# The gate and up products of a feed-forward block by one level of Strassen's scheme

## The chip, the core and the metric

The kernel runs on one core of a Trainium2 chip. The metric is the device time of one execution in microseconds (us). TensorE (PE in the rows) multiplies matrices into PSUM; VectorE (DVE), ScalarE (ACT) and GpSimd (POOL) work element by element; SyncE (SP) issues the transfers between DRAM and SBUF. Each engine runs its own list of instructions in order and waits at semaphores for the others.

## The reference

One decoder block for 1024 tokens of width 1024: two parallel mixers, a merge, an output product and a norm, and then the feed-forward part with which this change deals. In the reference's words:

```
h = h + rms_norm(mixed, mix_post_g[l])
u = rms_norm(h, ffn_pre_g[l])
gt, up = jnp.split(u @ w_ffn_in[l], 2, axis=-1)
h = h + rms_norm((jax.nn.silu(gt) * up) @ w_ffn_out[l], ffn_post_g[l])
```

`gt` and `up` are each 1024 x 2816, and `w_ffn_out` brings 2816 back to 1024. All is float32.

## The kernel before

Float32 products are made of three TensorE products each. An operand is split into a rounded high part and the remainder, its low part (`split`, line 83: ACT casts the high part at line 84, DVE subtracts it at line 85), and high x high, high x low and low x high are added in PSUM (`stat3`, line 101; `mov3`, line 106). A weight unit of 128 x 1024 is a DMA of 512 KB into `wr` and such a split into `wh` and `wl` (`unit`, line 87).

Before the feed-forward part stands the output product of the mixers (`wo_job`), for three sets of tokens (a "token" here is a block of 128): 0 to 2, 3 to 5, 6 and 7. While TensorE makes one set, `after` norms the tokens of the set before. For each token that is: sum of squares on ACT (line 981), the reciprocal root in two tiny POOL instructions (lines 97 and 98, tile `rs`), scale and residual on DVE (984, 985), `h2` to DRAM, sum of squares again (989), `rs` again, the scale to `n` on DVE (993), eight 128x128 transposes on TensorE (999), and the split of their results into `u2h` and `u2l`, which hold the normed activations transposed: 8 chunks of the width x 1024 tokens. Tokens 6 and 7 have no later set to hide behind. There `early` fills TensorE with 48 matmuls of hidden chunk 0, which need only tokens 0 to 3 (tile `f`).

The hidden width is 22 chunks of 128. For each chunk `gate_part` and `up_part` make a gate and an up product of 8 (chunks of the width) x 2 (token halves) x 3 = 48 matmuls 128x128 by 128x512, in the order of `chan_gen`: for each weight piece both token halves after one another. Silu (ACT, 1071), the product of gate and up (DVE, 1082) and its split follow. Every group of two chunks (the last has four) then passes through `out_part`, which multiplies it with `w_ffn_out` (line 1127) and adds the PSUM result to the accumulators `acc` on DVE (1114). The last group norms and writes the result.

Each engine's list is the order in which the program is written, with `drive` weaving a filler generator into the steps of a main one by numbers of nanoseconds. Nothing is rearranged later. So an instruction that stands in a list waits for all that stand before it there, also where it doesn't use their results.

Of the kernel before, what the change touches and what calls it, by code (L numbers as in the profile page):

```python
# [17 lines left out]
P = 128  # L18
D = 1024
# [23 lines left out]
def _f(ap):  # L43
    return ap.bitcast(F32)
# [3 lines left out]
def block_kernel(ctx: ExitStack, tc: tile.TileContext, a: dict, out: bass.AP, dbg=None):  # L48
# [84 lines left out]
    gb_d = dram("gb", [8, P, T])  # L133
    ma_d = dram("ma", [8, P, T])
    h2_d = dram("h2", [NT, P, D])

    HW = ((0, 512), (512, 1024))

# [767 lines left out]
    def yb_job(j):  # L906
        def run(w):
            gm, ma = io("gb"), io("ma")
            SP.dma_start(gm, gb_d[j])
            SP.dma_start(ma, ma_d[j])  # L910
            box = []
            yield from chan_gen(box, w, bh_, bl_)
            DVE.scalar_tensor_tensor(out=v2(gm), in0=v2(gm), scalar=1.0, in1=box[0], op0=ALU.add, op1=ALU.mult)
            DVE.tensor_tensor(out=gm, in0=gm, in1=ma, op=ALU.add)
            h_ = mp.tile([P, T], F32R, name=f"mh{j}", tag=f"mh{j}")
            l_ = mp.tile([P, T], F32R, name=f"ml{j}", tag=f"ml{j}")
            ACT.activation(h_, gm, AF.Copy, scale=0.5)
            DVE.scalar_tensor_tensor(out=l_, in0=gm, scalar=0.5, in1=_f(h_), op0=ALU.mult, op1=ALU.subtract)
            mh.append(h_)
            ml.append(l_)  # L920

        return (lambda: unit(a["wmo"][j])), run

# [7 lines left out]
    drain(G)  # L931
    pYa.close()
    bh_, bl_ = resident(ybp, ob_d, "b")
    pM = ExitStack()
    mp = pM.enter_context(tc.tile_pool(name="mp", bufs=1, reuse_waits="tile"))
    mh, ml = [], []
    drain(stream([yb_job(j) for j in range(8)]))
    pYb.close()


    fp = ctx.enter_context(tc.tile_pool(name="fp", bufs=1, side="right", reuse_waits="tile"))
    u2h = fp.tile([P, KC, T], F32R, name="u2h", tag="u2h")
    u2l = fp.tile([P, KC, T], F32R, name="u2l", tag="u2l")
    wo = pM.enter_context(tc.tile_pool(name="wo", bufs=1, reuse_waits="tile"))
# [4 lines left out]
    mix = {}  # L949

    def wo_job(toks, ch, k2, outs, spare):
        def run(w):
            wh, wl = (z.rearrange("p (k m) -> p k m", k=2) for z in w)
            if k2 == 0:
                if ch == 0:
                    b = [big("wo") for _ in range((len(toks) + 1) // 2)]
                    b = [z[:, i] for z in b for i in range(2)]
                    outs[:], spare[:] = b[: len(toks)], b[len(toks) :]
                else:
                    outs[:] = spare + [bank("wo2") for _ in toks[len(spare) :]]  # L960
            for i, t in enumerate(toks):
                xs = slice(t * P, (t + 1) * P)
                for k in range(2):
                    kc = 2 * k2 + k
                    mov3(outs[i], mh[kc][:, xs], ml[kc][:, xs], wh[:, k], wl[:, k], kc == 0, kc == KC - 1)
                if k2 == 3:
                    if ch == 0:
                        mix[t] = wo.tile([P, D], F32, name="mx", tag="mx", bufs=4)
                    ACT.copy(mix[t][:, 512 * ch : 512 * ch + 512], outs[i])
                yield 1290  # L970

        return (lambda: unit(a["wout"][ch, k2])), run

    def after(tok):
        m = mix.pop(tok)
        jk = u2l[:, :, tok * P : (tok + 1) * P]
        m8 = m.rearrange("p (k c) -> p k c", k=KC)
# [17 lines left out]
        c0 = tok * P  # L995
        for g in range(2):
            pt = bank("x2").rearrange("p (k c) -> p k c", c=P)
            for kc in range(4):
                PE.transpose(pt[:, kc], n[:, (4 * g + kc) * P : (4 * g + kc + 1) * P], ident)
            split(u2h[:, 4 * g : 4 * g + 4, c0 : c0 + P], u2l[:, 4 * g : 4 * g + 4, c0 : c0 + P], pt)  # L1000

    pipe = []

# [33 lines left out]
    def half_gen(w, b, e, o):
        wh, wl = (z.rearrange("p (k m) -> p k m", k=KC) for z in w)
        for kc in range(KC):
            stat3([o], wh[:, kc], wl[:, kc], [u2h[:, kc, b:e]], [u2l[:, kc, b:e]], kc == 0, kc == KC - 1)  # L1040
            yield 650

    w0 = [unit(a["wfg"][0]), unit(a["wfu"][0])]
    o0 = [big("f0") for _ in range(2)]
# [8 lines left out]
    for i in range(2):  # L1053
        drain(half_gen(w0[i], *HW[1], o0[i][:, 1]))
    pM.close()

    gp = ctx.enter_context(tc.tile_pool(name="gp", bufs=1, reuse_waits="tile"))
    acc = [gp.tile([P, D], F32, name=f"acc{t}", tag=f"acc{t}") for t in range(NT)]
    ends = list(range(GROUP, NH - 2 * GROUP + 1, GROUP)) + [NH]
    groups = [list(range(b, e)) for b, e in zip([0] + ends, ends)]  # L1060
    acts, sls = {}, {}

    def gate_part(j):
        s = gp.tile([P, 2, 512], F32, name="sl", tag="sl", bufs=2)
        if j == 0:
            o = o0[0]
        else:
            box = []
            drain(chan_gen(box, unit(a["wfg"][j]), halves(u2h), halves(u2l)))
            o = box[0]  # L1070
        ACT.activation(s, o, AF.Silu)
        sls[j] = s

    def up_part(j):
        s = sls.pop(j)
        if j == 0:
            o = o0[1]
        else:
            box = []
            drain(chan_gen(box, unit(a["wfu"][j]), halves(u2h), halves(u2l)))  # L1080
            o = box[0]
        DVE.tensor_tensor(out=s, in0=s, in1=o, op=ALU.mult)  # L1082
        ah = gp.tile([P, 2, 512], F32R, name="ah", tag="ah", bufs=4)
        al = gp.tile([P, 2, 512], F32R, name="al", tag="al", bufs=4)
        split(ah, al, s)
        acts[j] = ah, al

    def unit2(src):
        raw = wp.tile([P, 1024], F32, name="wr", tag="wr", bufs=3)
        hi = gp.tile([P, 1024], F32R, name="w2h", tag="w2h", bufs=2)  # L1090
        lo = gp.tile([P, 1024], F32R, name="w2l", tag="w2l", bufs=2)
        SP.dma_start(raw, src)
        split(hi, lo, raw)
        return hi, lo

    def out_part(gi):
        grp = groups[gi]
        last = gi == len(groups) - 1
        if last:
            gf = gp.tile([P, 2, 512], F32, name="sl", tag="sl", bufs=2)  # L1100
            SP.dma_start(gf.rearrange("p a c -> p (a c)"), a["ffn_post_g"].partition_broadcast(P))
        ws = [(unit2 if i < 2 else unit)(a["wfo"][j]) for i, j in enumerate(grp)]
        late = []
        for t in range(NT):
            bs = [bank("f2") for _ in range(2)]
# [4 lines left out]
            def add(ch):  # L1110
# [4 lines left out]
                if last:  # L1115
                    ACT.activation(jk[:, 512 * ch : 512 * ch + 512], av[ch], AF.Square, accum_out=s2[:, ch : ch + 1])

            pieces = ((0,), (1,)) if last and t == NT - 1 else ((0, 1),)
            for chs in pieces:
                for i, jj in enumerate(grp):  # L1120
                    xs = slice((t % 4) * P, (t % 4) * P + P)
                    ahs, als = (z[:, t // 4, xs] for z in acts[jj])
# [41 lines left out]
def _stationary(w):  # L1164
# [74 lines left out]
```

## Time and profile before

| | |
|---|---|
| median of 3 runs | 2064.35 us (2064.09 to 2065.51) |
| the profiled execution | 2065.24 us |
| its span (first to last instruction) | 2063.4 us |
| granted clock of TensorE, mean over the span | 0.997 of full speed |
| TensorE busy | 2029.8 us, 98% |
| VectorE, ScalarE, GpSimd busy | 979.6, 584.6, 81.6 us |
| DMA | 163 MB, 79 GB/s on average |
| end of the norms to the last matmul | 1330 to 2054.8 us of the span |

A stretch in which TensorE is busy all the time and its matmuls follow one another at an even distance is set by the number of matmuls. A stretch in which it waits is set by the chain of engines that it waits for. Rows of the trace give the start of an instruction, its duration, and in brackets the idle time before it with what ended it.

### The profile page before, as it was taken

How to read it: one execution, taken by the hardware profiler on the slowest of the kernel's cores; microseconds unless marked ns; L12 is line 12 of the kernel's file. 1: busy time of each engine (PE TensorE's matmuls, PEld its weight loads, DVE VectorE, ACT ScalarE, POOL GpSimd, SP SyncE). 2: the span in 40 equal slices, each digit the busy share in tenths (PEclk: the TensorE clock that was granted, in tenths of full speed). 3: DMA queues.
4: the chain of work that ended last, by engine and by line, in shares of the span. 5: the costliest groups of instructions: out<-in, count | busy, mean ns of one | idle time of the engine just before them, and what ended most of it. 6: DMA issues, size and time to landing. Idle time of an engine off the chain costs nothing.

```text
span 2063.4 us, 26451 instructions
## 1 busy us (share of the span) xinstructions
PE 2029.8 (98%) x11044; PEld 1753.0 (85%) x11044; DVE 979.6 (47%) x1707; ACT 584.6 (28%) x978; POOL 81.6 (4%) x149
## 2 busy tenths in 40 slices
PE   7999999999999999999999999999999999999998
PEld 7999998998888888888888887888888888888886
DVE  5456565555443335777762445731432334333326
ACT  5212111211213235555551214632111111111112
POOL 1000000000001100000000001200000000000002
PEclk9999999999999999999999999999999999999999
DMA  4111111021213033111145654621111111121014
GB/s 166 52 42 42 51 43 41 22 62 41 91 56 115 21 118 118 47 52 47 37 153 198 205 153 161 218 80 51 51 41 52 51 52 43 40 62 51 22 60 153
DMA packets 54151, 163.08 MB, mean 79 GB/s; under 512 B 5376, under 2 KB 14080, under 8 KB 54032
## 3 DMA queue, kind: packets, MB, share of 16 engines
q1 hardware_dynamic: 53888, 161.13, 23.8%
q8 instruction: 87, 1.43, 0.3%
q14 instruction: 32, 0.26, 0.0%
q10 hardware_dynamic: 144, 0.26, 0.0%
HBM read 127.82 MB, written 33.55 MB: 78 GB/s over the span
## 4 chain that ended last, share of the span: by engine, by line
PE 59%; issue 35%; DVE 2%; ACT 1%; POOL 1%; DMA 1%; SPq 0%; POOLq 0%; DVEq 0%; ACTq 0%
PE gm L104 25%; PE vb L108 6%; PE sb L750 3%; PE fb L104 3%; PE wo L108 3%; PE cb L108 3%; PE ov L811 2%; PE lv L367 2%; PE pT L798 1%; PE fg L104 1%; PE qn L104 1%; PE dg L306 1%; PE kn L104 1%; PE ob L427 1%; PE ob L426 1%
## 5 line engine op out<-in xcount | busy, mean ns | idle before, releaser
L84 ACT CAST wh<-wr 128x1024 fp32r<-128x1024 f32 (+1 forms) x143 | 148.7, 1040 | 695.3 <-PE gm L104 377.7
L85 DVE TENSOR_TENSOR wl<-wr,wh 128x1024 fp32r<-128x1024 f32 (+1 forms) x143 | 172.4, 1207 | 283.4 <-ACT wh L84 269.0
L104 PE MATMUL gm<-u2h,wl 128*128 128x512 f32 x672 | 206.9, 389 | 0.0
L104 PE MATMUL gm<-u2h,wh 128*128 128x512 f32 x672 | 206.9, 389 | 0.0
L104 PE MATMUL gm<-u2l,wh 128*128 128x512 f32 x672 | 206.9, 389 | 0.0
L104 PE MATMUL gm<-uh,wh 128*128 128x512 f32 x512 | 164.4, 402 | 0.0
L104 PE MATMUL gm<-uh,wl 128*128 128x512 f32 x512 | 158.3, 390 | 0.0
L104 PE MATMUL gm<-ul,wh 128*128 128x512 f32 x512 | 158.2, 390 | 0.0
L104 PEld LDWEIGHTS gm<-u2h,wl 128*128 128x128 f32 x672 | 126.2, 188 | 26.1
L104 PEld LDWEIGHTS gm<-u2h,wh 128*128 128x128 f32 x672 | 126.2, 188 | 26.1
L104 PEld LDWEIGHTS gm<-u2l,wh 128*128 128x128 f32 x672 | 126.2, 188 | 26.1
L1114 DVE TENSOR_TENSOR acc<-acc,f 128x512 f32<-128x512 f32 x144 | 92.5, 683 | 76.9 <-PE f L1127 76.9
L104 PEld LDWEIGHTS gm<-ul,wh 128*128 128x128 f32 x512 | 96.1, 188 | 20.5
L104 PEld LDWEIGHTS gm<-uh,wl 128*128 128x128 f32 x512 | 96.0, 188 | 20.5
L1082 DVE TENSOR_TENSOR sl<-sl,gm 128x1024 f32<-128x1024 f32 x21 | 25.6, 1221 | 174.1 <-PE gm L104 174.1
L104 PEld LDWEIGHTS gm<-uh,wh 128*128 128x128 f32 x512 | 92.8, 188 | 16.2
L1127 PE MATMUL f<-w2h,ah 128*128 128x512 f32 x320 | 98.9, 389 | 0.0
L1127 PE MATMUL f<-w2h,al 128*128 128x512 f32 x320 | 98.9, 389 | 0.0
L1127 PE MATMUL f<-w2l,ah 128*128 128x512 f32 x320 | 98.8, 389 | 0.0
L108 PE MATMUL vb<-wh,uh 128*128 128x256 f32 (+1 forms) x288 | 84.1, 292 | 0.0
L108 PE MATMUL vb<-wl,uh 128*128 128x256 f32 (+1 forms) x288 | 81.8, 284 | 0.1
L370 DVE COPY_PREDICATED AT<-masks,lv 128x128 f32<-128x128 uint8 x192 | 51.6, 322 | 63.9 <-PE lv L367 61.9
(329 smaller groups left out, 4029.4 us busy)
## 6 DMA issues: line engine op xcount, KB each, us to landing
wr<-in_wout SPq DMA_DIRECT2D x24, 512.0 KB, 3.5
wr<-in_wfg SPq DMA_DIRECT2D x22, 512.0 KB, 3.6
wr<-in_wfu SPq DMA_DIRECT2D x22, 512.0 KB, 3.4
wr<-in_wfo SPq DMA_DIRECT2D x22, 512.0 KB, 3.3
xt<-in_x SPq DMA_DIRECT2D x16, 512.0 KB, 4.8
wr<-in_wv SPq DMA_DIRECT2D x8, 512.0 KB, 3.6
wr<-in_whf SPq DMA_DIRECT2D x8, 512.0 KB, 3.7
wr<-in_whq SPq DMA_DIRECT2D x8, 512.0 KB, 3.6
```

Source lines behind the costliest of these rows:

```text
L84: ACT.copy(hi, src)
L85: DVE.tensor_tensor(out=lo, in0=src, in1=_f(hi), op=ALU.subtract)
L104: PE.matmul(o, w, x, start=first and j == 0, stop=last and j == 2)
L108: PE.matmul(o, x, w, start=first and j == 0, stop=last and j == 2)
L306: PE.matmul(b[:, c], k[:, (2 * g + c) * P : (2 * g + c + 1) * P], qq[:, 2 * g + c], start=True, stop=True)
L367: PE.matmul(b[:, :, c], k[:, cc * P : (cc + 1) * P], qx[:, :, cc], start=True, stop=True)
L370: DVE.copy_predicated(AT[:, 2 * g : 2 * g + 2].rearrange("p c (n w b) -> p (c n) w b", w=2, b=w)[:, :, 1], masks[:, j + s_ + (j > 2)].rear ...
L750: PE.matmul(o, x[:, qs], y[:, b0:e0], start=j == 0, stop=j == 4 and e0 <= d0)
L811: PE.matmul(ov[:, x], w, r[:, x], start=False, stop=kt == nkt - 1 and j == 2)
L1082: DVE.tensor_tensor(out=s, in0=s, in1=o, op=ALU.mult)
L1114: DVE.tensor_tensor(out=av[ch], in0=av[ch], in1=bs[ch], op=ALU.add)
L1127: PE.matmul(bs[ch], x, w[:, 512 * ch : 512 * ch + 512], start=f and j == 0, stop=l and j == 2)
```

## The change

**The products.** Hidden chunk j is paired with chunk j + 11, the two halves of the tokens (tokens 0 to 3 and 4 to 7) and the two halves of the width make a 2 x 2 grid, and a "chain" is one such pair for gate or for up: 22 chains. One level of Strassen's scheme in Winograd's form makes a chain of seven products instead of eight. A product is 4 (chunks of a half width) x 3 = 12 matmuls of 128x512 (`product`, line 1140 of the changed kernel), and several of the seven are added in the same PSUM bank: products 1, 6, 7, 4 in one half of `pa`, product 2 in the other, 5 and 3 in `pc`. In between, `post` copies intermediate results to SBUF on ACT and adds on DVE.

**The sums of weights.** Four sums or differences 128x512 for each chain (line 1111), on POOL for chains 0 and 1 (the gate and up of the first pair), on DVE for the other 20, and then the splits.

**The sums of activations.** For tokens 0 to 3 the normed `n` goes to DRAM as well (`n_d`). For tokens 4 to 7 `after` reads back the token four before into `no`, and POOL makes four differences 128x512 (line 1010, tiles `nt` and `no`); then 20 transposes (line 1022) instead of 8, five pairs of split instructions instead of two.

**The second product.** Silu(gate) x up goes to DRAM (`act_d`), and the product with `w_ffn_out` becomes a stage of its own after all chains; its operands are loaded and split one group ahead.

**The tiles of the mixers' output** are cut into three pools by token sets, so that each of the 8 merged chunks is cast in three pieces on ACT and three on DVE instead of one each.

On POOL, the list at the end of the norms stood as pairs of `rs` instructions. `no` and `nt` are the differences of activations (`n_11757` and `n_11831` are tokens 4 and 5, `n_11980` and `n_12044` tokens 6 and 7), `wr<-wr` the sums of weights:

```order
+L1111 TENSOR_TENSOR wr<-wr 128x512
 L97 TENSOR_SCALAR rs<-ss 128x1
 L98 TENSOR_TENSOR rs<-rs,mhalf 128x1
 L97 TENSOR_SCALAR rs<-ss 128x1
 L98 TENSOR_TENSOR rs<-rs,mhalf 128x1
+L1111 TENSOR_TENSOR wr<-wr 128x512
 L97 TENSOR_SCALAR rs<-ss 128x1
 L98 TENSOR_TENSOR rs<-rs,mhalf 128x1
+L1111 TENSOR_TENSOR wr<-wr 128x512 x2
+L1010 TENSOR_TENSOR nt<-n_11980,no 128x512
+L1010 TENSOR_TENSOR nt<-n_11980,nt 128x512
+L1010 TENSOR_TENSOR no<-nt,no 128x512
```

The three pairs of `rs` are the first norm of token 7, the second of token 6 and the second of token 7. Ahead of these rows stand the four differences of token 4 (with a pair of `rs` between them), the four of token 5, and four sums of weights with the first `rs` pair of token 6 among them; behind them the rest of token 6's differences and the four of token 7. So the `rs` pairs of tokens 6 and 7 now stand behind work on 128x512 tiles, and token 6's differences behind all eight sums of weights.

On TensorE, before, around the transposes of tokens 6 (`n_11854`) and 7 (`n_11887`):

```order
L104 MATMUL f_11798<-u2h,wl 128x512
L999 MATMUL x_11873<-ident,n_11854 128x128 x4
L999 MATMUL x_11880<-ident,n_11854 128x128 x4
L104 MATMUL f_11798<-u2h,wh 128x512
L104 MATMUL f_11798<-u2l,wh 128x512
L104 MATMUL f_11798<-u2h,wl 128x512
L104 MATMUL f_11798<-u2h,wh 128x512
L104 MATMUL f_11798<-u2l,wh 128x512
L104 MATMUL f_11798<-u2h,wl 128x512
L999 MATMUL x_11895<-ident,n_11887 128x128 x4
L999 MATMUL x_11902<-ident,n_11887 128x128 x4
L104 MATMUL f_11797<-u2h,wh 128x512
```

And in the changed kernel, from the last of the 48 matmuls that need no late token:

```order
L1140 MATMUL pa<-xbh,wl 128x512
L1022 MATMUL x_12009<-ident,n_11980 128x128 x4
L1022 MATMUL x_12016<-ident,nt 128x128 x4
L1022 MATMUL x_12023<-ident,nt 128x128 x4
L1022 MATMUL x_12030<-ident,no 128x128 x4
L1022 MATMUL x_12037<-ident,no 128x128 x4
L1022 MATMUL x_12061<-ident,n_12044 128x128 x4
L1022 MATMUL x_12068<-ident,nt 128x128 x4
L1022 MATMUL x_12075<-ident,nt 128x128 x4
L1022 MATMUL x_12082<-ident,no 128x128 x4
L1022 MATMUL x_12089<-ident,no 128x128 x4
L1140 MATMUL pc<-xth,wh 128x512
```

Before, 42 of the fillers stood ahead of token 6 and six between the two tokens. Now all 48 stand ahead of token 6, and the first matmul of product 5 (`pc`) stands behind the last transpose of token 7.

The diff, cut to its core:

```diff
-            h_ = mp.tile([P, T], F32R, name=f"mh{j}", tag=f"mh{j}")
-            l_ = mp.tile([P, T], F32R, name=f"ml{j}", tag=f"ml{j}")
...
+            for (b, e), (h_, l_) in mx_:
+                ACT.activation(h_[:, j], gm[:, b:e], AF.Copy, scale=0.5)
+                DVE.scalar_tensor_tensor(out=l_[:, j], in0=gm[:, b:e], scalar=0.5, in1=_f(h_)[:, j], op0=ALU.mult, op1=ALU.subtract)
...
         n = io("n2")
+        if tok >= 4:
+            o = io("no")
+            SP.dma_start(o, n_d[tok - 4])
         DVE.scalar_tensor_tensor(out=n, in0=m, scalar=r, in1=gpre, op0=ALU.mult, op1=ALU.mult)
+        if tok >= 4:
+            tt = io("nt")
+            o2, n2, t2 = (z.rearrange("p (a c) -> p a c", a=2) for z in (o, n, tt))
+            for out_, x, y in ((t2[:, 0], n2[:, 0], o2[:, 0]), (t2[:, 1], n2[:, 1], t2[:, 0]), (o2[:, 0], t2[:, 1], o2[:, 0]), (o2[:, 1], o2[:, 1], t2[:, 1])):
+                POOL.tensor_tensor(out=out_, in0=x, in1=y, op=ALU.subtract)
+        else:
+            SP.dma_start(n_d[tok], n)
         yield
...
+        def prep(self, part):
+            r0, r1 = (z.rearrange("p (a c) -> p a c", a=2) for z in self.raw)
+            sub = lambda o, x, y, op=ALU.subtract: (POOL if self.n < 2 else DVE).tensor_tensor(out=o, in0=x, in1=y, op=op)
+            if part == 0:
+                self.put(self.raw[0], (1, 2))
+            elif part == 1:
+                z = raw_tile()
+                self.s12 = z.rearrange("p (a c) -> p a c", a=2)
+                sub(self.s12[:, 0], r1[:, 0], r1[:, 1], ALU.add)
+                sub(self.s12[:, 1], self.s12[:, 0], r0[:, 0])
+                self.put(z, (5, 6))
+            elif part == 2:
+                z = raw_tile()
+                s34 = z.rearrange("p (a c) -> p a c", a=2)
+                sub(s34[:, 0], r0[:, 0], r1[:, 0])
+                sub(s34[:, 1], r0[:, 1], self.s12[:, 1])
+                self.put(z, (7, 3))
+            else:
+                self.put(r1[:, 1], (4,))
...
+            for k in range(HK):
+                for j, (w, x) in enumerate(((wh, xh), (wh, xl), (wl, xh))):
+                    PE.matmul(o, w[:, k], x[:, k], start=fresh and k == 0 and j == 0, stop=k == HK - 1 and j == 2, skip_group_check=not fresh)
+                yield 680
+            self.post(i)
...
+    c0.load()
+    for i in range(3):
+        c0.prep(i)
+    c1.load()
+    c1.prep(0)
...
     def early():
-        for i in range(2):
-            yield from half_gen(w0[i], *HW[0], o0[i][:, 0])
+        for c in (c0, c1):
+            yield from c.product(1)
+            yield from c.product(2)
...
+            c.prep(1)
+            yield from c.product(1)
+            yield from chains[n - 1].product(4)
+            c.prep(2)
+            if not last:
+                chains[n + 1].load()
+            yield from c.product(2)
+            yield from c.product(5)
+            c.prep(3)
+            yield from c.product(6)
+            if not last:
+                chains[n + 1].prep(0)
+            yield from c.product(3)
+            yield from c.product(7)
...
-    for gi, grp in enumerate(groups):
-        for i, j in enumerate(grp):
-            gate_part(j)
-            if i == 0 and gi:
-                out_part(gi - 1)
-            up_part(j)
-    out_part(len(groups) - 1)
+    for gi in range(len(groups)):
+        out_part(gi)
```

`put` splits a tile and keeps its two halves as the left operands of two products; `load` reads the two weight chunks of a chain; `big` has two buffers of two PSUM banks, `bank` four of one, and `io` (which holds `n`, `no`, `nt` and the gate tiles) is a ring of SBUF tiles that are used again in turn.

## Rows read from the trace of the kernel before

**Rows 1.** Page, first part: busy us, share of the span, instructions.

```profile
PE 2029.8 (98%) x11044; PEld 1753.0 (85%) x11044; DVE 979.6 (47%) x1707; ACT 584.6 (28%) x978; POOL 81.6 (4%) x149
```

**Rows 2.** Stretches: length, then the columns that the first line names.

```profile
core 0: us, PE busy (x) PEld busy (x) DVE busy (x) ACT busy (x) POOL busy (x), PEclk, DMA share, GB/s
1320.00:1333.00 13.00, 13.00 (x70) 10.99 (x69) 11.51 (x12) 9.23 (x15) 1.25 (x2) 1.00 0.91 324
...
1358.30:2012.00 653.70, 653.70 (x2885) 541.51 (x2884) 204.14 (x231) 112.96 (x118) 0.00 (x0) 1.00 0.15 48
```

**Rows 3.** FFN products, groups by line and shape: busy us, mean ns, idle us.

```profile
L1114 DVE TENSOR_TENSOR acc<-acc,f 128x512 f32<-128x512 f32 x144 | 92.5, 683 | 76.9 <-PE f L1127 76.9
...
L85 DVE TENSOR_TENSOR wl<-wr,wh 128x1024 fp32r<-128x1024 f32 x43 | 52.5, 1222 | 166.7 <-ACT wh L84 166.7
L84 ACT CAST wh<-wr 128x1024 fp32r<-128x1024 f32 x43 | 45.3, 1054 | 371.7 <-PE gm L104 232.0 <-issue 136.4 <-PE f L104 3.3
...
L1071 ACT ACTIVATE sl<-gm 128x1024 f32<-128x1024 f32 x21 | 21.3, 1014 | 0.0
```

**Rows 4.** TensorE in order of time, end of the norms: start, duration.

```profile
1330.18 1.03 PE L999 MATMUL x<-ident,n 128*128 128x128 f32 x8
...
1333.54 0.40 PE L104 MATMUL f<-u2l,wh 128*128 128x512 f32 x1
...
1342.62 0.39 PE L104 MATMUL f<-u2h,wl 128*128 128x512 f32 x1
1342.89 1.06 PE L999 MATMUL x<-ident,n 128*128 128x128 f32 x8
...
1346.45 0.73 PE L104 MATMUL f<-u2h,wh 128*128 128x512 f32 x2 [0.24 <-ACT u2h L84]
```

**Rows 5.** VectorE in order of time, the same place.

```profile
1321.83 1.28 DVE L993 SCALAR_TENSOR_TENSOR n<-mx,rs,gpre 128x1024 f32<-128x1024 f32 x1
...
1335.13 1.28 DVE L85 TENSOR_TENSOR u2l<-x,u2h 128x512 fp32r<-128x512 f32 x2
...
1337.46 1.28 DVE L984 SCALAR_TENSOR_TENSOR mx<-mx,rs,gpost 128x1024 f32<-128x1024 f32 x1
1338.66 1.22 DVE L85 TENSOR_TENSOR wl<-wr,wh 128x1024 fp32r<-128x1024 f32 x1
1339.80 1.22 DVE L985 TENSOR_TENSOR mx<-mx,xt 128x1024 f32<-128x1024 f32 x1
```

**Rows 6.** GpSimd in order of time, the same place.

```profile
1323.58 0.71 POOL L97 TENSOR_SCALAR rs<-ss 128x1 f32<-128x1 f32 x1 [4.73 <-ACT u2l L989]
...
1335.84 0.55 POOL L98 TENSOR_TENSOR rs<-rs,mhalf 128x1 f32<-128x1 f32 x1
1338.88 1.05 POOL L97 TENSOR_SCALAR rs<-ss 128x1 f32<-128x1 f32 x1 [2.49 <-ACT u2l L989]
1340.01 1.41 POOL L98 TENSOR_TENSOR rs<-rs,mhalf 128x1 f32<-128x1 f32 x1
```

**Rows 7.** GpSimd's widest operation in the whole span, by line and shape.

```profile
L474 POOL CAST masks<-tt 128x896 uint8<-128x896 f32 x1 | 0.9, 929 | 0.0
```

**Rows 8.** ScalarE groups of the norms and splits, by line and shape.

```profile
L84 ACT CAST u2h<-x 128x512 fp32r<-128x512 f32 x16 | 8.6, 595 | 1.5 <-PE x L999 1.5
...
L989 ACT ACTIVATE u2l<-mx 128x1024 fp32r<-128x1024 f32 x8 | 8.5, 1062 | 10.0 <-DVE mx L985 8.3 <-POOL rs L97 1.8
```

**Rows 9.** Page, sixth part: DMA issues, count, KB each, median us to landing.

```profile
wr<-in_wfu SPq DMA_DIRECT2D x22, 512.0 KB, 3.4
```

**Rows 10.** TensorE in order of time where its clock rises at the start.

```profile
17.55 0.40 PE L108 MATMUL vb<-wh,ul 128*128 128x256 f32 x1
17.76 0.30 PE L108 MATMUL vb<-wh,uh 128*128 128x256 f32 x1
17.90 0.28 PE L108 MATMUL vb<-wl,uh 128*128 128x256 f32 x1
18.02 0.28 PE L108 MATMUL vb<-wh,ul 128*128 128x256 f32 x1
```

More of the change, by code (lines that the diff above doesn't have):

```diff
@@ L949, in block_kernel, with wide @@
     mix = {}
+    sums = []
+    def wide(name):
+        return wo.tile([P, D], F32, name=name, tag="mx", bufs=4)
     def wo_job(toks, ch, k2, outs, spare):
@@ L1028, in block_kernel @@
     drain(stream(wo_jobs(sets[0])))
+    pM[0].close()
     G = stream(wo_jobs(sets[1]))
@@ L1031, in block_kernel @@
     drain(G)
+    pM[1].close()
+    tp = tp_.enter_context(tc.tile_pool(name="tp", bufs=1, side="right", reuse_waits="tile"))
+    sums[:] = (tp.tile([P, 4, HK, 512], F32R, name=z, tag=z) for z in ("xth", "xtl"))
     G = stream(wo_jobs(sets[2]))
@@ L1034, in block_kernel, with raw_tile @@
     drain(G)
[L1037 to L1044, printed above, removed]
+    pM[2].close()
+    wq = ctx.enter_context(tc.tile_pool(name="wq", bufs=1, reuse_waits="tile"))
+    made = {"r": 0, "u": 0}
+    def raw_tile():
+        made["r"] += 1
+        if made["r"] % 5 < 3:
+            return wp.tile([P, 1024], F32, name="wr", tag="wr", bufs=3)
+        return wq.tile([P, 1024], F32, name="wr", tag="wr", bufs=2)
@@ L1052, in block_kernel, with rest @@
     drain(G)
[L1053 to L1058, printed above, removed]
+    def rest():
+        yield from c0.product(5)
+        c0.prep(3)
+        yield from c0.product(6)
+        c1.prep(1)
+        yield from c0.product(3)
+        yield from c0.product(7)
+        c1.prep(2)
+        chains[2].load()
+        yield from c1.product(5)
+        c1.prep(3)
+        yield from c0.product(4)
+        yield from c1.product(6)
+        chains[2].prep(0)
+        yield from c1.product(3)
+        yield from c1.product(7)
+        for n in range(2, 2 * NP_):
+            c, last = chains[n], n == 2 * NP_ - 1
+            c.prep(1)
[12 more added lines that the diff above has]
+            yield from c.product(7)
+        yield from chains[-1].product(4)
@@ L1088, in unit2, with second @@
[L1088 to L1092, printed above, removed]
-        split(hi, lo, raw)
-        return hi, lo
+    held = {}
+    def second(j, kind, tiles):
+        raw = raw_tile()
+        SP.dma_start(raw, (act_d if kind == "a" else a["wfo"])[j])
+        hi, lo = tiles()
+        split(hi, lo, raw)
+        held[kind, j] = hi, lo
@@ new lines, in block_kernel, with ring @@
+    R = rest()
+    steps = 4 * (7 * 2 * NP_ - 4) - 12
+    for _ in range(steps):
+        next(R)
+    second(0, "a", unit_tiles)
+    drain(R)
+    for kind, j in (("w", 0), ("a", 1), ("w", 1)):
+        second(j, kind, unit_tiles)
+    tp_.close()
+    xp_.close()
+    gp = ctx.enter_context(tc.tile_pool(name="gp", bufs=1, side="right", reuse_waits="tile"))
+    acc = [gp.tile([P, D], F32, name=f"acc{t}", tag=f"acc{t}") for t in range(NT)]
+    def ring():
+        return [gp.tile([P, 1024], F32R, name=z, tag=z, bufs=8) for z in ("vh", "vl")]
@@ L1098, in out_part @@
         last = gi == len(groups) - 1
+        todo = [] if last else [(j, kind) for j in groups[gi + 1] for kind in "aw"]
         if last:
-            gf = gp.tile([P, 2, 512], F32, name="sl", tag="sl", bufs=2)
+            gf = wide("gf").rearrange("p (a c) -> p a c", a=2)
             SP.dma_start(gf.rearrange("p a c -> p (a c)"), a["ffn_post_g"].partition_broadcast(P))
-        ws = [(unit2 if i < 2 else unit)(a["wfo"][j]) for i, j in enumerate(grp)]
+        xs_ = [held.pop(("a", j)) for j in grp]
+        ws = [held.pop(("w", j)) for j in grp]
         late = []
@@ L1116, in add @@
                     ACT.activation(jk[:, 512 * ch : 512 * ch + 512], av[ch], AF.Square, accum_out=s2[:, ch : ch + 1])
+            for _ in range(2 if len(todo) > 4 or t % 2 == 0 else 0):
+                if todo and t < 7:
+                    second(*todo.pop(0), ring)
             pieces = ((0,), (1,)) if last and t == NT - 1 else ((0, 1),)
             for chs in pieces:
[L1120 to L1122 removed]
+                for i in range(len(grp)):
+                    xs = slice(t * P, (t + 1) * P)
+                    ahs, als = (z[:, xs] for z in xs_[i])
                     f, l = i == 0, i == len(grp) - 1
```

150 lines of the change are left out of this document (106 added, 44 removed).

## The prediction, made before the changed kernel ran

> **What bounds the kernel now.** I read the page's first part, then the table of stretches, then the groups by line, then the three engines in order of time where the norms end. TensorE is busy 98% of the span [rows 1]. From 1358 us to 2012 us it is busy in every microsecond: 2885 matmuls in 653.7 us, one every 0.2266 us, while VectorE works 31% of that time, ScalarE 17%, GpSimd not at all, and the DMA engines 15% [rows 2]. So the feed-forward products are bound by the number of matmuls, and a matmul taken away there is worth 0.2267 us. Before that stretch lies a different place. When the output product of the mixers ends (1330.18, transposes of token 4 [rows 4]) TensorE lives on 48 fillers until the last tokens are normed, and the main work starts at 1346.45. Today the fillers cover that chain almost to the end: the wait at 1346.45 is 0.24 us [rows 4]. There VectorE is nearly full, 11.5 of 13 us, and the DMA engines 91% [rows 2].
>
> **Matmuls removed.** Before: 22 chunks x 2 x 48 = 2112 for gate and up. After: 22 chains x 7 products x 12 = 1848. The second product stays at 22 x 8 x 2 x 3 = 1056. So 264 fewer, 264 x 0.2267 = 59.85 us, all on the path. A product accumulates in one bank, where before two banks took turns. The fillers `f` also stay in one bank: 1333.54 to 1342.62 for 40 of them, 0.227 us each [rows 4], so the price of one matmul doesn't change.
>
> **Hand-overs in the chains.** A gate chain takes 84 x 0.2267 = 19.0 us of TensorE. VectorE: four weight sums at 0.68, three and a half low halves at 1.22, three adds at 0.68, 9 us; for an up chain four multiplications at 0.68 more, 12 us. ScalarE: three and a half casts at 1.05, three copies at 0.59, Silu 2.0 for a gate, 7.5 us [rows 3, 8]. Neither is a bound. The tightest hand-over is the copy after product 6, which product 7 waits for since it adds in the same bank: product 3 lies between, 12 x 0.2267 = 2.72 us, and ScalarE answers in 0.59, or in 1.65 if it has just begun a cast. I cost these at nothing; the cover is that one product, and without it each chain would pay some 1.7 us. The second product as a stage needs per group of two chunks 96 matmuls, 21.8 us, against four low halves and sixteen adds on VectorE, 15.8 us [rows 3]; again nothing. Its first operands are loaded within the last chains; for that seam and the one at the end I take 1 us. The extra transfers (22 x 512 KB out and in) come to 35 GB/s beside 48 in a stretch with a DMA share of 15% [rows 2]: nothing. The finer casts of the mixers' output add two short instructions on each of two engines per chunk, beside 48 matmuls (10.9 us): nothing.
>
> **The end of the norms** is where the change costs. It puts 24 instructions of 128x512 on GpSimd (sixteen differences of activations, eight sums of weights), in one line with the `rs` pairs that the norms wait for, and lets TensorE run all 48 fillers first. The trace has no two-input operation of that size on GpSimd. Its widest is a one-input cast, 896 elements in 0.929 us, 1.04 ns per element [rows 7]. At that rate 512 elements take 0.53 us; with two inputs read one after the other, 1.06. A third bound is a difference that first waits for a whole VectorE instruction of 1.28 us [rows 5], 2.34 together. I take 1.06, the rate of the only wide row with both inputs counted, and keep 0.53 and 2.34.
>
> The path, by these rows, with the order of the lists:
> - The `n` of token 4 ends at 1321.83 + 1.28 = 1323.1 [rows 5]. Four differences with the `rs` of token 5 between them (0.71 and 0.55 [rows 6]): 1328.6. Token 5's four: 1332.9.
> - Three sums of weights, `rs` of token 6 (0.19 and 0.55 [rows 6]) with a fourth sum inside: 1337.8. Only now is the transfer of the next weight chunk issued, since it reuses the tile that this sum frees; 3.4 us [rows 9]: 1341.2. The fifth sum waits for it, and the `rs` of token 7 stands behind: 1343.0.
> - VectorE has the scale of token 7 ahead of the residual of token 6, so both tokens wait: 1.28 + 1.22 [rows 5], 1345.5. Square on ScalarE 1.06 [rows 8], `rs` 0.74: 1347.3.
> - The sixth sum, `rs` of token 7, two sums: 1351.3. Token 6's four differences: 1355.5.
> - The `n` of token 7 reuses a tile which those four read, and on VectorE stands behind the split of their transposes (0.4 + 0.60 + 0.64 [rows 4, 5, 8]): 1357.1, then 1.28: 1358.4. Four differences: 1362.7. Four transposes: 1363.2, product 5.
>
> All 24 GpSimd instructions lie on this path, 25.4 us of its 40. Nothing fills TensorE: the 48 fillers (10.9 us) are used up early, and every transpose stands behind them. To it comes contention. An `rs` pair takes 0.19 + 0.55 us alone or beside a split that reads PSUM, as at 1335.84 beside the split of 1335.13. Beside VectorE's instructions with two inputs in SBUF, at 1338.66 and 1339.80, it takes 1.05 + 1.41 [rows 5, 6]: 0.86 more in each. Six low halves of weights, all with two inputs in SBUF, lie off the path in this stretch: 6 x 0.86 = 5.2 us. With some 0.1 us at each of about ten changes of engine: 1369.9. Against 1346.45 that is 23.5 us lost. The 24 additional transposes of tokens 6 and 7 are inside it; those of tokens 4 and 5 run while GpSimd is the later one.
>
> [...]
>
> After such a wait TensorE's clock is at its lower level at first. [...] Between none and all twelve of product 5 I take seven: 1.3 us (0 to 2.2).
>
> **Sum**, against the profiled execution's 2065.24 us: - 59.85 + 23.5 + 1.3 + 1.0 = 2031.2. That execution is 0.9 above the median of the runs, so 2030 us.
>
> **Rivals.**
> *A shorter wait.* At 0.53 us per GpSimd instruction the path loses 24 x 0.53 = 12.7 us: 2018. With everything hidden only the 48 transposes at 0.13 us stay: 2065.2 - 59.9 + 6.2 - 0.9 = 2011. For it: TensorE reads nothing of GpSimd's but these tiles. Against: two inputs, and the waits for the transfer and for the tile of `n` remain at any speed. 2011 to 2022.
> *GpSimd shut out by VectorE.* If each of the 24 first waits for an instruction of 1.28 us, + 30.7: 2061. For it the doubled `rs` rows and VectorE at 88% [rows 2]; against it that VectorE stands on this path itself and can't run beside all of them. 2042 to 2061.
> *The chains wait (the other side).* ScalarE's list holds, ahead of the copies that free a bank, casts of weight sums which wait for VectorE, and VectorE's sums stand behind adds that wait for a product. If that ring closes, TensorE pays in every chain. The 35 us won are gone at 35 / 22 = 1.6 us per chain; at 2 us it is 2030 + 44 = 2074. For it: seven dependent hand-overs where before a product of 48 matmuls had another bank pair free. Against it: 1.1 us of room at the tightest, 7 us of idle VectorE and 11 of ScalarE per chain. From 2069.
> *The change doesn't do what it says.* Matmuls that add to a bank of another product could cost more than 0.2267 us: 1848 x 0.02 = 37 us would undo it, and the time would stay near 2065. The `f` rows speak against it [rows 4].
>
> **Chances.** The forecast (2022 to 2042, its own range) 0.62; shorter wait 0.20; shut out 0.10; chains that wait 0.06; no effect 0.02. A difference under 0.2% (4 us) can't be told from no change here. Faster by more than that: 0.62 + 0.20 + 0.10 = 0.92; same 0.02; slower 0.06. From 2014 to 2048 some 0.16 is left out: a little at 2011 to 2014, the upper part of "shut out", and the last two cases.
>
> **What would show it.** In the changed kernel's trace: an even 0.227 us between matmuls in the chains, with no wait of TensorE at the seven hand-overs; a hole of TensorE between the last filler and product 5, 1341 to about 1370, which ends with a transpose that waits for GpSimd; differences of about 1.06 us there, longer beside VectorE's two-input instructions; the `rs` of token 7 behind a sum that waits for a DMA; the granted clock below full for the first matmuls after the hole. It would be wrong if the hole ended before 1360 or after 1380, or if TensorE waited by more than a few tenths of a microsecond per chain.

## The result and the profile after

The changed kernel takes 2038.18 us (median of 4 runs, 2037.56 to 2039.92) against 2064.22 in the same comparison: ratio 0.9875, 95% interval 0.9858 to 0.9892. That is 26 us faster; 34 were forecast.

The page's first part, for the whole span (2036.9 us):

```profile
PE 1986.1 (98%) x10828; PEld 1712.4 (84%) x10828; DVE 1130.6 (56%) x1947; ACT 666.0 (33%) x1138; POOL 116.7 (6%) x173
```

Against [rows 1]: 216 matmuls fewer (264 products taken away, 48 transposes added), VectorE and GpSimd with more work. Then the hole and the stretches from the chains to the end, with [rows 2]'s columns:

```profile
core 0: us, PE busy (x) PEld busy (x) DVE busy (x) ACT busy (x) POOL busy (x), PEclk, DMA share, GB/s
1341.00:1380.00 39.00, 22.86 (x82) 15.93 (x81) 25.83 (x27) 17.39 (x27) 26.47 (x23) 0.68 0.27 95
1380.00:1790.00 410.00, 410.00 (x1805) 339.27 (x1804) 212.62 (x271) 139.73 (x194) 0.00 (x0) 1.00 0.25 87
1790.00:2025.00 235.00, 235.00 (x1037) 194.12 (x1036) 152.85 (x207) 56.11 (x82) 8.68 (x18) 1.00 0.33 112
```

TensorE is busy in every microsecond of the last two: 1805 matmuls in 410 us and 1037 in 235 us are 0.2271 and 0.2266 us each, as before. The list of TensorE's waits has no entry from 1380 us on. So the seven hand-overs of each chain, the seam to the second product (matmuls of both stand side by side at 1786 us) and the transfers cost nothing that the trace shows. From the start of product 5 there are 1848 - 48 + 1056 = 2856 matmuls, 647.5 us at 0.2267; 1379.07 plus that plus 1.5 us of lower clock (below) is 2028.1, and the last matmul starts at 2028.17. All that the change lost, it lost before 1380 us. There, on TensorE, where [rows 4] had one wait of 0.24 us:

```profile
1346.41 0.80 PE L1140 MATMUL pa<-xbh,wh 128*128 128x512 f32 x1 [4.70 <-ACT wh L84]
...
1358.51 0.60 PE L1022 MATMUL x<-ident,n 128*128 128x128 f32 x4
1364.69 1.12 PE L1022 MATMUL x<-ident,nt 128*128 128x128 f32 x4 [5.57 <-POOL nt L1010]
...
1372.76 1.09 PE L1022 MATMUL x<-ident,n 128*128 128x128 f32 x4 [2.68 <-DVE n L1005]
...
1377.08 2.34 PE L1022 MATMUL x<-ident,no 128*128 128x128 f32 x8 [0.23 <-POOL no L1010]
1379.07 0.78 PE L1140 MATMUL pc<-xth,wh 128*128 128x512 f32 x1
```

The main work starts at 1379.07 instead of 1346.45, 32.6 us later. The waits in brackets end with GpSimd's `nt` (5.57 us for token 6), with the `n` of token 7 on VectorE, and, already among the fillers, with a cast of weights on ScalarE (4.70): a cast at 1342.45 had waited 4.58 us for one of GpSimd's sums of weights, and the casts that product 1 of the next chain needs stand behind it. The transposes at 1364.69 take 1.1 us for four where those at 1358.51 took 0.6: the clock has fallen, from a granted 1.00 (1358.5 to 1359.2 us) to 0.50 (1364.6 to 1365.9 us). The granted clock of 1341 to 1380 us is 0.68 on average in the table of stretches. Product 5 starts at a granted clock of 0.52 (1379.07 to 1382.13 us):

```profile
1379.65 0.63 PE L1140 MATMUL pc<-xtl,wh 128*128 128x512 f32 x1
1380.07 0.63 PE L1140 MATMUL pc<-xth,wl 128*128 128x512 f32 x1
...
1381.78 0.51 PE L1140 MATMUL pc<-xth,wh 128*128 128x512 f32 x1
1382.13 0.40 PE L1140 MATMUL pc<-xtl,wh 128*128 128x512 f32 x1
```

0.43 us between matmuls at the lower level, 0.23 again from 1382.13 on, at a granted clock of 1.00 (1382.2 to 1400 us); the seven intervals up to there take 3.06 us instead of 1.59.

GpSimd, where [rows 6] had only `rs` pairs:

```profile
1323.46 1.30 POOL L1010 TENSOR_TENSOR nt<-n,no 128x512 f32<-128x512 f32 x1 [2.06 <-DMA wr<-in_wout]
...
1325.97 2.15 POOL L1010 TENSOR_TENSOR nt<-n,nt 128x512 f32<-128x512 f32 x1
...
1336.17 1.28 POOL L1010 TENSOR_TENSOR no<-nt,no 128x512 f32<-128x512 f32 x1
...
1342.77 1.26 POOL L1111 TENSOR_TENSOR wr<-wr 128x512 f32<-128x512 f32 x1
...
1347.45 2.27 POOL L1111 TENSOR_TENSOR wr<-wr 128x512 f32<-128x512 f32 x1 [1.92 <-DVE wl L85]
1349.80 1.05 POOL L97 TENSOR_SCALAR rs<-ss 128x1 f32<-128x1 f32 x1
...
1362.39 2.24 POOL L1010 TENSOR_TENSOR nt<-n,no 128x512 f32<-128x512 f32 x1
1364.71 1.27 POOL L1010 TENSOR_TENSOR nt<-n,nt 128x512 f32<-128x512 f32 x1
...
1376.98 1.27 POOL L1010 TENSOR_TENSOR no<-no,nt 128x512 f32<-128x512 f32 x1
```

A difference or sum takes 1.26 to 1.30 us alone, 2.15 to 2.27 beside a 128x1024 instruction of VectorE with two inputs in SBUF, and 1.6 beside a 128x512 one (1366.06 and 1372.74). All 24 together take 36.3 us (16 differences 23.9, the eight sums 12.4 by the groups), 1.51 us each. In the kernel before, an `rs` instruction takes this long alone, the price from which the prediction counts its delay of 0.86 us:

```profile
1335.57 0.19 POOL L97 TENSOR_SCALAR rs<-ss 128x1 f32<-128x1 f32 x1 [1.67 <-ACT u2l L981]
```

And VectorE is held up as well, where [rows 5] had 1.22 and 1.28 for the same instructions:

```profile
1328.96 2.02 DVE L85 TENSOR_TENSOR wl<-wr,wh 128x1024 fp32r<-128x1024 f32 x1
...
1348.51 2.30 DVE L993 SCALAR_TENSOR_TENSOR mx<-mx,rs,gpost 128x1024 f32<-128x1024 f32 x1
...
1363.44 0.68 DVE L85 TENSOR_TENSOR xbl<-x,xbh 128x512 fp32r<-128x512 f32 x1
...
1371.34 1.27 DVE L1005 SCALAR_TENSOR_TENSOR n<-mx,rs,gpre 128x1024 f32<-128x1024 f32 x1
```

The low half of 1328.96 and the scale of 1348.51 run beside GpSimd's instructions; the split of 1363.44 reads PSUM and keeps its 0.68 us beside the difference of 1362.39.

### The profile page after: what moved, and what is told of

It is laid out like the page before. It is cut to its first block, busy times and chain, and to the rows that moved or that the text cites. A ratio compares the mean times of both kernels' runs of the same rounds, so it can differ in the third digit from the quotient of the medians.

```text
span 2036.9 us, 26832 instructions
## 1 busy us (share of the span) xinstructions
PE 1986.1 (98%) x10828; PEld 1712.4 (84%) x10828; DVE 1130.6 (56%) x1947; ACT 666.0 (33%) x1138; POOL 116.7 (6%) x173
## 5 line engine op out<-in xcount | busy, mean ns | idle before, releaser
L85 DVE TENSOR_TENSOR wl<-wr,wh 128x1024 fp32r<-128x1024 f32 (+1 forms) x189 | 218.6, 1158 | 250.9 <-ACT wh L84 236.1
L1140 PE MATMUL pa<-xth,wh 128*128 128x512 f32 x264 | 102.8, 389 | 0.0
L1140 PE MATMUL pa<-xtl,wh 128*128 128x512 f32 x264 | 102.7, 389 | 0.0
L1140 PE MATMUL pa<-xth,wl 128*128 128x512 f32 x264 | 102.7, 389 | 0.0
L1301 PE MATMUL f<-vl,vh 128*128 128x512 f32 x320 | 99.2, 389 | 0.0
L1301 PE MATMUL f<-vh 128*128 128x512 f32 x320 | 99.2, 389 | 0.0
L1301 PE MATMUL f<-vh,vl 128*128 128x512 f32 x320 | 99.1, 389 | 0.0
L108 PE MATMUL vb<-wh,ul 128*128 128x256 f32 (+1 forms) x288 | 81.5, 283 | 0.0
L1140 PE MATMUL pa<-xbh,wh 128*128 128x512 f32 x176 | 70.0, 398 | 5.9 <-ACT wh L84 4.7
L1301 PEld LDWEIGHTS f<-vl,vh 128*128 128x128 f32 x320 | 60.1, 188 | 12.6
```

Source lines behind the costliest of these rows:

```text
L85: DVE.tensor_tensor(out=lo, in0=src, in1=_f(hi), op=ALU.subtract)
L108: PE.matmul(o, x, w, start=first and j == 0, stop=last and j == 2)
L1140: PE.matmul(o, w[:, k], x[:, k], start=fresh and k == 0 and j == 0, stop=k == HK - 1 and j == 2, skip_group_check=not fresh)
L1301: PE.matmul(bs[ch], x, w[:, 512 * ch : 512 * ch + 512], start=f and j == 0, stop=l and j == 2)
```

## The experiments

Theory G is that of the prediction: GpSimd's list, with the norms' `rs` pairs in it, sets the end of the wait. Its main rival V: VectorE has as much to do there, and sets it as soon as GpSimd doesn't. Each kernel is compared with the kernel before on the same chip, whose median is 2063.9 to 2064.3 us in all of these comparisons; the changed kernel is 2038.2 us.

**The sums of weights to VectorE.**

```diff
-            sub = lambda o, x, y, op=ALU.subtract: (POOL if self.n < 2 else DVE).tensor_tensor(out=o, in0=x, in1=y, op=op)
+            sub = lambda o, x, y, op=ALU.subtract: DVE.tensor_tensor(out=o, in0=x, in1=y, op=op)
```

> The eight sums of weights of the first two chains go from GpSimd to VectorE; the differences of activations stay on GpSimd. Theory G (GpSimd's list sets the end of the wait, 24 instructions one after the other with the norms' rs pairs among them): eight of 24 leave, 1.26 us or more each against about 0.6 on VectorE, and the rs pair of token 7 no longer stands behind a sum that waits for a transfer; product 5 starts 9 to 12 us earlier, 2026 to 2029 us. Rival V (VectorE is the bound there: it is busy 26 of the 39 us of the wait, and what it gets in addition it must do there): within 3 us of the changed kernel, 2035 to 2038 us.

Measured: 2034.65 us (2033.02 to 2035.01), product 5 at 1374.44, 4.6 us earlier. A gain, but less than half of what G expects, and a little more than V's.

**The differences of activations to VectorE.**

```diff
-                POOL.tensor_tensor(out=out_, in0=x, in1=y, op=ALU.subtract)
+                DVE.tensor_tensor(out=out_, in0=x, in1=y, op=ALU.subtract)
```

> The sixteen differences of activations go from GpSimd to VectorE; the sums of weights stay on GpSimd. Theory G: sixteen of the 24 leave, they took 1.26 to 2.26 us each, 23 us in all, and take about 0.6 each on VectorE, 10 us: product 5 starts 10 to 14 us earlier, 2024 to 2028 us. Rival V: VectorE gets 10 us more where it has 13 us free in the wait, and half of those are waits for others: 2033 to 2038 us. Rival O (only the order counts: the rs pair behind the sum that waits for a transfer): that stays, so 2034 us or more.

Measured: 2038.41 us (2036.59 to 2039.92), product 5 at 1379.08: nothing gained. Theory G's size falls here: two thirds of the 24 instructions left GpSimd, and the end stayed. V's and O's ranges both allow it. GpSimd's and VectorE's rows of this kernel:

```profile
1334.64 0.19 POOL L97 TENSOR_SCALAR rs<-ss 128x1 f32<-128x1 f32 x1 [9.46 <-ACT xtl L990]
...
1335.43 6.35 POOL L1111 TENSOR_TENSOR wr<-wr 128x512 f32<-128x512 f32 x4
1345.42 1.27 POOL L1111 TENSOR_TENSOR wr<-wr 128x512 f32<-128x512 f32 x1 [3.64 <-ACT xth L84]
1346.77 1.05 POOL L97 TENSOR_SCALAR rs<-ss 128x1 f32<-128x1 f32 x1
1347.90 1.41 POOL L98 TENSOR_TENSOR rs<-rs,mhalf 128x1 f32<-128x1 f32 x1
```

```profile
1346.31 2.59 DVE L85 TENSOR_TENSOR wl<-wr,wh 128x1024 fp32r<-128x1024 f32 x2
1348.83 2.47 DVE L993 SCALAR_TENSOR_TENSOR mx<-mx,rs,gpost 128x1024 f32<-128x1024 f32 x2
```

The `rs` pair of token 7 (1346.77) stands behind five sums, the last of which waits 3.64 us, as rival O has it; with both on VectorE (next) the same pair runs at 1337.42. But up to there it isn't what the norms wait for. The `rs` of token 6 was ready at 1335.5, and VectorE comes to its scale (L993) only at 1348.83, since from 1332 on it is busy but for some 0.6 us (22.13 us of the 25 from 1332 to 1357, with nothing to do from 1354.77 on); the `rs` of token 7, ready at 1349.3, is in time for the second scale, which follows without a gap. Up to there it is V that holds.

**Both to VectorE.** The two edits together.

> Differences and sums both on VectorE, GpSimd only makes the rs pairs. Theory G: the two gains add, product 5 18 to 24 us earlier, 2014 to 2020 us. Rival V: VectorE has 26 us of work in the wait and gets 24 x 0.6 = 14 more, 40 us in 39: no better than the better of the two alone, 2024 to 2030 us.

Measured: 2029.71 us (2028.66 to 2032.27), product 5 at 1369.70. The two edits don't give G's 18 to 24 us but 9.4 us of product 5; the time is at the upper end of V's range. It is more than the gains of the two alone, 3.5 and 0 us, which fits two bounds close to each other. VectorE's list leaves almost no gap:

```profile
1339.07 2.68 DVE L85 TENSOR_TENSOR xtl<-x,xth 128x512 fp32r<-128x512 f32 x4
1341.67 1.89 DVE L1111 TENSOR_TENSOR wr<-wr 128x512 f32<-128x512 f32 x3
1343.47 1.28 DVE L993 SCALAR_TENSOR_TENSOR mx<-mx,rs,gpost 128x1024 f32<-128x1024 f32 x1
1344.67 1.22 DVE L85 TENSOR_TENSOR wl<-wr,wh 128x1024 fp32r<-128x1024 f32 x1
```

The `rs` of token 6 was ready at 1335.1 (GpSimd has nothing else to do), and VectorE comes to the scale that waits for it (L993) at 1343.47, behind splits and three sums. The stretch from 1332 to 1357 us in four of the kernels, first the changed one, then with both on VectorE:

```profile
1332.00:1357.00 25.00, 18.20 (x83) 13.39 (x82) 18.95 (x21) 14.63 (x27) 17.12 (x17) 0.86 0.36 124
```

```profile
1332.00:1357.00 25.00, 19.31 (x92) 14.38 (x91) 23.36 (x31) 16.74 (x28) 3.82 (x8) 0.93 0.37 127
```

VectorE is busy 19.0 us of these 25 in the changed kernel and 23.4 here (third figure after the length), GpSimd 17.1 and 3.8.

**The sums of chain 0 later in the program**, behind product 1 of chain 1.

```diff
-    for i in range(3):
-        c0.prep(i)
-    c1.load()
+    c0.zs = [raw_tile(), raw_tile()]
+    c0.prep(0)
+    c1.load_half(0)
     c1.prep(0)
...
+        yield from c1.product(1)
+        c0.prep(1)
+        yield from c1.product(2)
+        c0.prep(2)
+        c1.load_half(1)
```

> Both on VectorE, and the sums of chain 0 and the load of the second weight chunk of chain 1 stand later in the program (after product 1 of chain 1), so that fewer of them come ahead of the norms. Theory G says that GpSimd no longer matters here and only order on VectorE is left: 2010 to 2018 us, 2 to 5 us under the kernel with both on VectorE. Rival V: the work on VectorE until product 5 is the same, product 5 needs two of the sums, so within 2 us of the kernel with both on VectorE.

Measured: 2028.32 us (2027.26 to 2029.31), product 5 at 1368.30. 1.4 us, as V expects, and the two ranges of runs overlap: this change of order did little while VectorE's work stayed the same.

**The differences left out**, with both on VectorE.

```diff
-            tt = io("nt")
-            o2, n2, t2 = (z.rearrange("p (a c) -> p a c", a=2) for z in (o, n, tt))
+            n2 = n.rearrange("p (a c) -> p a c", a=2)
+            o2 = t2 = n2
             for out_, x, y in (...):
-                DVE.tensor_tensor(out=out_, in0=x, in1=y, op=ALU.subtract)
+                pass
```

> Sums of weights on VectorE, and the sixteen differences of activations left out with the transfers that bring the earlier tokens back: the 20 transposes read the normed tokens themselves, so gate and up are not the reference's. Against the kernel with both on VectorE (2029.7 us, product 5 at 1369.7, VectorE without a gap of more than 1.4 us from 1331.6 on). Theory V (the sum of VectorE's work sets the end of the wait): twelve differences at 0.6 us lie in that stretch, 7.2 us less: product 5 at 1362 to 1363, 2021 to 2024 us. Rival L (a chain of latencies from engine to engine sets it, VectorE is only busy beside it): of the chain only the four differences of token 7 and the transfer go, 2.4 us at most: 2027 to 2030 us.

Measured: 2018.51 us (2017.82 to 2018.70), product 5 at 1359.41, 10.3 us earlier, more than V's 7.2 and far more than L's 2.4. The 3 us beyond V are not taken apart here. With the differences also goes what hung on them: the transfer, and the place of token 7's `n` on VectorE, which starts at 1361.96 behind token 6's differences and splits with them and at 1353.28 without.

```profile
1332.00:1357.00 25.00, 20.89 (x115) 15.81 (x113) 23.44 (x31) 19.25 (x33) 2.96 (x8) 1.00 0.24 88
```

VectorE is as full as with them (23.4 of 25 us), only done sooner. That speaks for its work and against rival L as it was priced; since the order on VectorE changed too, it doesn't exclude that part of the gain is a shorter chain.

**The differences of tokens 4 and 5 back to GpSimd**, which is free then.

```diff
-                DVE.tensor_tensor(out=out_, in0=x, in1=y, op=ALU.subtract)
+                (POOL if tok < 6 else DVE).tensor_tensor(out=out_, in0=x, in1=y, op=ALU.subtract)
```

> As the kernel with late sums on VectorE (2028.3 us), but the differences of tokens 4 and 5 back on GpSimd. Theory V: eight differences at 0.6 us leave VectorE where it is full, 4.8 us: 2023 to 2025 us. Rival P (a GpSimd difference beside VectorE's instructions with two inputs in SBUF holds VectorE up by as much as it takes from it: 1.22 became 2.0 to 2.3 in the changed kernel's trace): no gain or a loss, 2028 to 2034 us.

Measured: 2026.23 us (2025.75 to 2026.60), product 5 at 1365.34: 2.1 us of V's 3.3 to 5.3. Some 1.8 us of the rest can be rival P: two low halves on VectorE beside these differences take 2.01 and 2.24 us instead of 1.22.

**Sums behind the residual of token 7.** The same, with the sums put behind that instruction in VectorE's list.

> As the one before, and all sums of weights of the first two chains are issued on VectorE behind the residual of token 7. Theory V: the work until product 5 is smaller by the sums of the later products, about 2 to 4 us: 2020 to 2023 us. Rival (order and volume hardly change, product 5 now waits for the split of its own weights): within 2 us of the one before.

Measured: 2026.47 us (2025.55 to 2026.92), no difference: the rival. TensorE waits 1.3 us for the split weights of product 5 instead.

**Sums on GpSimd as well.**

> Differences of tokens 4 and 5 and the late sums of weights on GpSimd, differences of tokens 6 and 7 on VectorE: the smallest load of VectorE in any of these. Theory V: eight sums at 0.6 us leave VectorE as well, 2019 to 2022 us. Theory G (GpSimd's list with the rs pairs behind 1.26 us instructions): four sums stand ahead of or between the rs pairs of tokens 6 and 7, 5 us later norms: 2026 to 2031 us.

Measured: 2031.28 us (2031.17 to 2032.31), product 5 at 1373.17, 5 us worse, although VectorE is busy 24.0 us from 1331 to 1360 us where it was 27.0 with the late sums on VectorE. That is theory G: on GpSimd four sums, from 1340.31 to 1347.2, stand ahead of and between the `rs` pairs of tokens 6 and 7. Both bounds are real; which one decides depends on where the work is.

**The low halves off VectorE.** TensorE waits there anyway. For tokens 5 to 7 it subtracts the high half in PSUM, and ScalarE copies the low half out.

```diff
-            split(hi, lo, pt)
+            if tok < 5:
+                split(hi, lo, pt)
+            else:
+                ACT.copy(hi, pt)
+                PE.matmul(pt, nid, hi, start=False, stop=True, skip_group_check=True)
+                ACT.copy(lo, pt)
```

`nid` is a negative identity. Two kernels have this edit as it stands, a third has it for tokens 6 and 7 only. In all three each of the four transposes into a bank starts the bank anew, so minus the high half is added to the last of the four tiles alone and replaces the other three (the numbers for that stand in the last section). Their results are therefore not the reference's; their instructions are as many and of the same shapes.

> As the kernel with differences 4 and 5 on GpSimd and late sums on VectorE (2026.2 us), but for tokens 5 to 7 the low halves of the transposed tiles leave VectorE: TensorE adds minus the high half to the transposes in PSUM (one 128x512 matmul with a negative identity), and ScalarE copies the rest out. Theory V (VectorE's work sets the end): fifteen subtractions at 0.6 us leave it, 9 us: 2017 to 2020 us. Rival A (ScalarE takes over: fifteen copies at 0.59 more where it is busy 18 of 29 us, and each split becomes a chain of three engines): 2022 to 2027 us.

Measured: 2024.04 us (2023.26 to 2025.39), product 5 at 1363.85: 2.2 us, rival A's range.

> The same low halves by TensorE and ScalarE, on the kernel with all differences and late sums on VectorE (2028.3 us). Theory V: 9 us less: 2018 to 2021 us, 1 to 3 us above the one with differences 4 and 5 on GpSimd, since VectorE has their eight instructions more. Theory G (GpSimd's differences hold up the rs pairs of tokens 6 and 7, which matters once VectorE is free): equal or below it. Rival A: 2022 to 2027 us.

Measured: 2019.49 us (2018.91 to 2019.99), product 5 at 1360.39: 8.8 us, and 4.6 below the one with differences 4 and 5 on GpSimd. Theory G's condition shows in the other one: there VectorE waits 2.15 us for the `rs` of token 6 behind the differences, and the `n` of tokens 6 and 7 come 1.2 and 2.0 us later than here. What makes up the rest of the 4.6 is not taken apart.

> The same as the first of these, for tokens 6 and 7 alone; TensorE's additional matmuls then all lie in its wait. Theory V: ten subtractions at 0.6 us, 6 us: 2020 to 2022 us, 2 to 3 us above the first. Rival A: if ScalarE is the bound, below the first, since it has five copies less.

Measured: 2023.74 us (2022.25 to 2024.48), the same as the first of the three (product 5 at 1362.08). Five tiles more or fewer off VectorE make no difference where GpSimd has the differences of tokens 4 and 5; neither V nor A alone tells that.

**The four transposes as one group**, in the second of these three kernels:

```diff
-                PE.transpose(pt[:, kc], src[:, kc * P : (kc + 1) * P], ident)
+                if tok < 5:
+                    PE.transpose(pt[:, kc], src[:, kc * P : (kc + 1) * P], ident)
+                else:
+                    PE.matmul(pt[:, kc], src[:, kc * P : (kc + 1) * P], ident, start=kc == 0, stop=True, is_transpose=True, skip_group_check=True)
```

> The kernel with all differences and late sums on VectorE and the low halves of tokens 5 to 7 by TensorE and ScalarE, with one edit: of the four transposes into a bank only the first starts the bank anew, so that minus the high half is added to all four and the result is the reference's. Theory V: the same work in the same places, 2018 to 2021 us, about 18 us under the changed kernel. Rival: if TensorE adds by reading PSUM first, transposes that don't start a bank anew are slower and product 5 starts later, 2022 us or more.

Measured: 2018.36 us (2017.72 to 2018.97), ratio to the kernel before 0.9782, interval 0.9768 to 0.9795. Product 5 starts at 1357.92, and the waits of TensorE from 1300 us to 1400 us are short:

```profile
PE wo L108 <- DVE wl L85: 0.7, 1, 0.7
PE pa L1159 <- ACT t L1183: 0.7, 1, 0.7
PE x L1030 <- ACT xth L1029: 0.6, 3, 0.3
PE x L1025 <- ACT mx L976: 0.6, 1, 0.6
PE x L1025 <- DVE nt L1010: 0.4, 1, 0.4
```

```profile
1332.00:1357.00 25.00, 22.57 (x119) 16.62 (x117) 24.28 (x33) 24.24 (x44) 4.99 (x8) 1.00 0.51 169
```

3.0 us of waits in all, where the changed kernel had 18.6. The rival's slower transposes don't show. The granted clock is full (1.00, last but two), and so are VectorE and ScalarE, 24.3 and 24.2 of 25 us. Of the 32.6 us of the changed kernel 11.5 remain against 1346.45. That is about TensorE's own additional work, 48 transposes at 0.13 us [rows 4] and fifteen matmuls at 0.23, and the waits. By this estimate what is left to win there needs less work and not another order.

## Why the prediction was right, and where its terms were off

- **The matmuls removed, 59.85 us.** Right: 0.227 us between matmuls throughout, in one bank as in two.
- **Hand-overs, second product, seam: 0 + 1 us.** Right; the seam cost at most some tenths. The rival that chains wait did not occur, nor a dearer matmul.
- **The end of the norms, 23.5 us.** The right place and the right engines, too small: 32.6 us. The hole ended at 1379.07, 0.9 us short of the 1380 beyond which the prediction called itself wrong. (Its printed terms add up to 1369.4 and not 1369.9.) The chain ran in the order written; its times drift apart by 5.8 us when token 5's differences end (1338.7 against 1332.9), 7.4 at the fifth sum (1349.7 against 1342.3), 13.4 at the end of token 6's differences (1368.9 against 1355.5), all before the allowance for contention. Two terms were mis-sized. The larger is the operation: taken at 1.06 us from a one-input cast, it is 1.27 alone, which is 24 x 0.21 = 5.0 us against the 9.1 that are missing. The other is contention: six delays of 0.86 us were allowed, 5.2 in all, while in the trace the 24 instructions take 36.3 us instead of 24 x 1.27 = 30.5 and three `rs` instructions among them 0.86 to 0.99 us longer each, 8.5 in all. VectorE's own delay (1.22 us became 2.0) was not counted. Not all of these need lie on the path; how much of the 9.1 each made is not taken apart.
- **Two of its signs.** The fifth sum did wait, 1.92 us. The transfer that the prediction named was issued at 1344.06, when the fourth sum freed the tile, and landed 3.2 us later; by the trace the wait ended some 0.2 us after that, with a low half on VectorE. But the fillers were not used up by 1341: the first twelve end there, and the other 36 run from 1346.41 to 1358.5, behind the wait of 4.70 us for a cast, for which the prediction had no term. By the trace it cost nothing, since TensorE then waited for GpSimd until 1364.69.
- **Shut out by VectorE.** This rival put a whole instruction of VectorE ahead of each of the 24, 30.7 us. In the trace they are 5.8 us longer than alone.
- **The lower clock, 1.3 us.** Some 0.19 us more for each of seven matmuls was the author's estimate, and no run shows it: in [rows 10] the distance between matmuls of 256 columns falls from 0.21 to 0.12 us, but the granted clock is 1.00 both before that (15.2 to 17.7 us) and after (17.7 to 20 us), so that it isn't shown that the clock rises there. What the changed kernel shows is 0.43 us between matmuls instead of 0.227 at a granted clock of 0.52, over seven intervals 1.5 us. The lower clock also slowed the transposes in the hole, 1.1 us for four instead of 0.6, for which there was no term.
- **The delay of 0.86 us.** It was read from 128x1 instructions. The GpSimd instructions of 1325.97, 1347.45 and 1362.39, 128x512, end 1.1 us after the low half of VectorE beside them, a little less than their own length of 1.27. VectorE's instruction had begun earlier, and they take 2.15, 2.27 and 2.24 us: the delay is 0.88 to 1.0 us, near the 0.86 of the `rs` rows.
- **What the prediction said of the cause goes too far.** It put the wait down to the GpSimd instructions on the path. The runs show two bounds close to each other: GpSimd's list with the `rs` pairs in it, and VectorE's work. Moving sixteen of 24 instructions off GpSimd won nothing; moving all won 8.5 us; and only taking work off VectorE too won 20.
- **One sentence ahead of the prediction is not so.** "Nothing is rearranged later" doesn't hold: the program writes the transposes of token 5 ahead of all matmuls of the chains, and in the changed kernel's list a matmul of product 1 (1336.88) stands between them. What orders the lists is not shown here. The rows of the lists that were quoted, and the path, are from the lists themselves.

## What to carry to other kernels

A saving on the engine that is the bound is real where that engine is busy without a gap, and the loss is to be looked for where it waits: here a scheme that adds element-wise work won 60 us in the steady state and lost 33 in one place, the end of the norms. For such a place add up each engine's work until the waited-for instruction, not only the path: the next engine was almost as full, so relieving one alone gave little. Here the work was best moved to what had room in that place, the waiting TensorE and ScalarE, and it won 8.8 us with GpSimd's list clear and 2.2 with differences left there.

## What the runs showed of the hardware

- In the changed kernel a GpSimd instruction on 128x512 with two inputs in SBUF takes 1.26 to 1.30 us. Where it meets a 128x1024 instruction of VectorE with two inputs in SBUF, the one that starts later takes longer, up to 2.27 us on GpSimd (1347.45) and 2.30 on VectorE (1348.51; VectorE's take 1.22 and 1.28 alone).
- A 128x512 instruction of VectorE with one input in PSUM keeps its 0.68 us beside GpSimd's of 128x512 in the same trace (1363.44).
- In the kernel with low halves by TensorE and all differences on VectorE, a GpSimd instruction of 128x1 that takes 0.19 us alone took 3.35 at 1338.32, beside four instructions of VectorE with two inputs in SBUF that followed one another (1338.00 to 1341.62); it ended with the last of them.
- Where each of the four transposes starts its bank anew, only the last of them is added to here; the later matmul that should add replaces the other three. The outputs of the kernels with that for tokens 5 to 7 and for 6 and 7 differ from the reference's by 0.9325 and 0.7611 of its norm. The block calculated from the reference with the first three tiles of each four cancelled gives these two numbers; with nothing subtracted from the three, it would give 0.53 and 0.43. With only the first of the four starting the bank, all four are added to, and the transposes are not slower by the time of the kernel (2018.36 against 2019.49 us).
